# Expert weights in 2 MB units with 16 KB runs, and what that moves elsewhere in a two-block network

## The chip, the cores and the metric

The kernel runs on one core of a Trainium2 chip. The metric is the device time of one execution in microseconds (us). Before the change the median of three runs is 2280.82 us (2279.59 to 2280.99). All numbers are f32 in memory; products that choose experts are formed from a high and a low part of each weight, so that f32 accuracy is kept.

## The reference

256 tokens of width 1024 go through `first_block` (two layers of attention and feed-forward) and then `second_block` (a gated recurrence, a gated unit over chunks, a projection by `w_out`, and a layer of 16 experts), followed by a last RMSNorm. The change concerns the experts; each expert picks the 32 tokens with the largest share for it:

```python
def moe_expert_choice(h, router_w, w_gate, w_up, w_down):
    cap = CAPACITY_FACTOR * T // N_EXPERTS                      # 2 * 256 / 16 = 32
    aff = jax.nn.softmax((h @ router_w).astype(jnp.float32), axis=-1)
    gate, idx = lax.top_k(jnp.swapaxes(aff, 1, 2), cap)
    xs = h[bidx, idx]
    hid = jax.nn.silu(jnp.einsum('becd,edf->becf', xs, w_gate)) * jnp.einsum('becd,edf->becf', xs, w_up)
    ye = jnp.einsum('becf,efd->becd', hid, w_down) * gate[..., None].astype(h.dtype)
    return jnp.zeros_like(h).at[bidx, idx].add(ye)
...
        x = x + g_m * y                                         # y ends in the product by w_out
        h2 = modulate_2(rmsnorm_2(x, norm_ffn_w[l]), sh_f, sc_f)
        x = x + g_f * moe_expert_choice(h2, router_w[l], expert_w_gate[l], expert_w_up[l], expert_w_down[l])
    return rmsnorm_2(x, final_norm_w)
```

Each expert has three matrices of 8 MB (1024 x 2048, 1024 x 2048, 2048 x 1024): 403 MB in all, of 625 MB that the kernel moves.

## The kernel before

**Weights of everything but the experts.** `Weights` brings them in blocks of 1 MB into two buffers, `raw` (L101). ScalarE casts a block into `wh`, its high part (L396), VectorE forms `wl`, the low part, as the difference (L403), and TensorE multiplies with both (`mm3` and `gemm_T`; three matmuls per product, L485 to 487 and L503 to 505). The parts live in the pool `pair`, three buffers of `wh` and three of `wl`, 1 MB each. `more(n)` casts up to n blocks ahead and then calls `fetch(1)`, which may send one unit of expert weights.

**Expert weights.** `experts` lists them as 1 MB units in the order of use: for each expert eight k blocks of gate, eight of up, and eight of down. A unit of gate or up is 128 rows of 2048, one row (8 KB) to a partition; a unit of down is 256 rows, two rows (8 KB together) to a partition. The last four units, the second half of the last expert's down matrix, hold 512 columns each, in runs of 2 KB. `fetch` (DMA at L2196) goes round a ring of `slots`, which grows when other things are freed: `xw0` (4), `xw1` (2), then the two `raw` and six `pair` buffers, then `xw2` (5), 19 MB in all. While other weights still load, one unit goes out behind each `more`; when the last block of `w_out` has been taken, and again when the second block is done, `fetch()` sends all for which there is a slot. After that each `take()`, called before the matmuls of a unit, frees the slot of the unit before and sends one more.

All these DMAs, and those of `raw`, are sent by SyncE (SP) in program order, one after the other. SyncE waits, ahead of a DMA, for the semaphore of the one eight back and, where a buffer is written again, for its last reader.

**Ahead of the experts.** The end of the second block (`block2`) multiplies `merged` by `w_out` in four 1 MB blocks (kk, c), two token tiles each. `route` is a generator that is advanced between them. Its first step, `route_weights`, folds scale and shift into the router's weights on VectorE: `A2f` (the scale of the norm, 128 x 8, L658), `rb`, `rw` (L2223 to 2225). It is placed ahead of the first `w_out` product. After the last product come the router's logits, softmax, `moe`'s selection of 32 tokens for each expert, and `gather(0)`, which forms the first 512 features of all chosen tokens (`xsA`) by a product with a selection matrix `S`; scale and shift (`A2f` and a piece of `modc`) are applied where the result leaves PSUM. `gather(1)` forms the other half (`xB`) before the fifth k block of the first gate matrix.

**Experts.** For each unit of gate or up TensorE runs four matmuls (L2400), 32 tokens stationary, 512 columns of the unit moving, one for each quarter of the partitions of a PSUM bank, so that a bank holds 4 x 32 partitions of 512 columns. `columns` transposes the gated hidden layer back into columns, and L2418 (for the last four units L2428) multiplies with down. `scatter` adds an expert's output into the tokens while the next expert's gate runs. The hidden layer of the last expert is transposed twice, once for either way of reading down.

## Time and profile before

| | |
|---|---|
| median of three runs | 2280.82 us (2279.59 to 2280.99) |
| the profiled execution | 2285.08 us |
| its span, first to last instruction | 2283.2 us |
| mean granted clock of TensorE | 0.879 of full speed |
| TensorE busy | 1903.5 us, 83% |
| VectorE / ScalarE / GpSimd busy | 934.9 / 620.2 / 222.5 us |
| bytes moved | 625.48 MB in 182796 packets, mean 274 GB/s |
| the experts' DMAs | sent 19.8 to 19.9 us before they land, 1024 KB each |

The engines are PE (TensorE matmul), PEld (its weight load), DVE (VectorE), ACT (ScalarE), POOL (GpSimd) and SP (SyncE; SPq is its DMA queue). Busy shares are means over stages with different limits, so a stage is read by itself: by a window (busy time of each engine, granted clock and DMA in a stretch), by the timeline of an engine (instructions one after the other, with what ended the idle time before each), by the waits, and by the chain that ended last. [...]

### The profile page before, as it was taken

What the parts mean: (1) busy time and instruction counts of PE and PEld (TensorE: products, weight loads), DVE (VectorE), ACT (ScalarE), POOL (GpSimd) and SP (SyncE); (2) the same over time, 40 slices, a digit from 0 to 9 for tenths busy, and PEclk for the clock granted to TensorE, in tenths of its full rate; (3) what the DMA queues carried; (4) which work ended last, traced back from release to release, by engine and by line L of the source; (5) the groups of instructions that cost most, each with busy time, mean ns of one, the idle gap of its engine ahead of it and who ended that gap; (6) DMA issues with size and microseconds to landing.
All of it is one profiled execution on the core that took longest, in us unless ns stands there. A gap on an engine that the chain in (4) does not pass through costs nothing. (4 is left out here: it accounts for less than half of the span.)

```text
span 2283.2 us, 26558 instructions
## 1 busy us (share of the span) xinstructions
PE 1903.5 (83%) x10872; PEld 1166.0 (51%) x10872; DVE 934.9 (41%) x1400; ACT 620.2 (27%) x964; POOL 222.5 (10%) x282
## 2 busy tenths in 40 slices
PE   7999899999999999999979987676666666667665
PEld 4865688788778778999868751111111111111111
DVE  4547645687556765755578631000000000000001
ACT  3336433222134665644566420000000000000001
POOL 1001030111113001000242010000000000000000
PEclk8999999999999999999989987767777777777777
DMA  8446235776742234555434789999999999999998
GB/s 320 142 140 215 90 123 183 270 237 213 244 152 65 68 118 148 196 194 168 149 125 141 269 349 421 420 421 421 421 421 420 421 421 421 421 421 421 421 421 328
DMA packets 182796, 625.48 MB, mean 274 GB/s; under 512 B 17384, under 2 KB 77730, under 8 KB 130962
## 3 DMA queue, kind: packets, MB, share of 16 engines
q1 hardware_dynamic: 167792, 572.70, 64.9%
q0 software_dynamic: 14480, 50.63, 6.6%
q8 instruction: 86, 1.41, 0.3%
q10 hardware_dynamic: 402, 0.45, 0.1%
q14 instruction: 36, 0.29, 0.0%
HBM read 622.63 MB, written 1.10 MB: 273 GB/s over the span
## 5 line engine op out<-in xcount | busy, mean ns | idle before, releaser
L403 DVE TENSOR_TENSOR wl<-raw,wh 128x2048 fp32r<-128x2048 f32 (+3 forms) x141 | 293.1, 2083 | 234.4 <-ACT wh L396 231.4
L396 ACT CAST wh<-raw 128x2048 fp32r<-128x2048 f32 (+2 forms) x132 | 231.0, 1756 | 203.1 <-PE ps L504 102.2
L505 PE MATMUL ps<-hx,wl 128*128 128x256 f32 (+1 forms) x848 | 272.0, 321 | 3.9 <-DVE wl L403 3.8
L503 PE MATMUL ps<-hx,wh 128*128 128x256 f32 (+1 forms) x848 | 273.5, 323 | 0.0
L504 PE MATMUL ps<-lx,wh 128*128 128x256 f32 (+1 forms) x848 | 272.1, 321 | 0.9 <-DVE lx L720 0.7
L413 ACT COPY GT<-ps 128x256 f32<-128x256 f32 x16 | 6.0, 372 | 879.8 <-PE ps L2345 879.8
L2410 DVE TENSOR_TENSOR s<-s,gu 128x512 f32<-128x512 f32 x16 | 11.0, 687 | 478.0 <-ACT s L2409 478.0
L505 PEld LDWEIGHTS ps<-hx,wl 128*128 128x128 f32 x848 | 159.8, 188 | 17.2 <-DVE wl L403 4.8
L503 PEld LDWEIGHTS ps<-hx,wh 128*128 128x128 f32 x848 | 159.9, 189 | 14.7 <-issue 2.5
L504 PEld LDWEIGHTS ps<-lx,wh 128*128 128x128 f32 x848 | 159.9, 189 | 13.9 <-DVE lx L720 1.4
L2400 PE MATMUL gu<-xw,xB 128*32 128x512 f32 x584 | 107.2, 821 | 60.7 <-DMA xw<-in_expert_w_gate 30.7
L2400 PE MATMUL gu<-xw,xsA 128*32 128x512 f32 x584 | 106.9, 829 | 42.8 <-DMA xw<-in_expert_w_up 31.4
L2418 PE MATMUL ye<-xw,ehT 128*32 128x512 f32 x592 | 102.0, 812 | 47.1 <-DMA xw<-in_expert_w_down 39.3
L567 DVE SCALAR_TENSOR_TENSOR acc<-av,s,acc 128x1024 f32<-128x1024 f32 x84 | 106.1, 1281 | 40.2 <-DMA av<-in_ada_w 39.5
L2357 DVE TENSOR_TENSOR s<-gf,ye 128x512 f32<-128x512 f32 x32 | 20.6, 684 | 248.9 <-PE ye L2418 236.9
L485 PE MATMUL ps<-wh,hidh 128*128 128x512 f32 x264 | 104.3, 395 | 0.0
L487 PE MATMUL ps<-wh,hidl 128*128 128x512 f32 x264 | 103.7, 393 | 0.0
L486 PE MATMUL ps<-wl,hidh 128*128 128x512 f32 x264 | 103.5, 392 | 0.0
L2341 POOL TENSOR_TENSOR SG<-S,aff 128x128 f32<-128x128 f32 x32 | 12.1, 399 | 820.3 <-PE ps L2345 820.3
L2400 PEld LDWEIGHTS gu<-xw,xB 128*32 128x32 f32 x584 | 13.8, 123 | 147.1 <-DMA xw<-in_expert_w_up 79.7
L485 PE MATMUL ps<-wh,hx 128*128 128x512 f32 (+2 forms) x208 | 81.6, 392 | 6.9 <-ACT ST L1909 6.0
L486 PE MATMUL ps<-wl,hx 128*128 128x512 f32 (+2 forms) x208 | 79.9, 384 | 3.1 <-POOL wl L402 1.9
(566 smaller groups left out, 3258.2 us busy)
## 6 DMA issues: line engine op xcount, KB each, us to landing
xw<-in_expert_w_down SPq DMA_DIRECT2D x77, 1024.0 KB, 19.9
xw<-in_expert_w_gate SPq DMA_DIRECT2D x75, 1024.0 KB, 19.8
xw<-in_expert_w_up SPq DMA_DIRECT2D x71, 1024.0 KB, 19.8
raw<-in_ffn_w SPq DMA_DIRECT2D x64, 1024.0 KB, 5.1
av<-in_ada_w POOLq DMA_DIRECT2D x80, 512.0 KB, 5.2
raw<-in_w_in SPq DMA_DIRECT2D x28, 1024.0 KB, 5.1
araw<-in_ada_w SPq DMA_DIRECT2D x24, 1024.0 KB, 4.7
wl<-in_expert_w_up SPq DMA_DIRECT2D x22, 1024.0 KB, 19.9
```

Of the source, the lines that this page charges most:

```text
L396: self.nc.scalar.copy(hi, src)
L403: self.nc.vector.tensor_sub(lo[:, n:], src[:, n:], hi[:, n:].bitcast(F32))
L485: nc.tensor.matmul(o, lhsT=a, rhs=w[0][:, j, :], start=k0 + j == 0, stop=False)
L486: nc.tensor.matmul(o, lhsT=a, rhs=w[1][:, j, :], start=False, stop=False)
L487: nc.tensor.matmul(o, lhsT=b, rhs=w[0][:, j, :], start=False, stop=k0 + j == nk - 1)
L503: nc.tensor.matmul(out, lhsT=a, rhs=xh[:, k, n0:n0 + n], start=k == 0, stop=False)
L504: nc.tensor.matmul(out, lhsT=a, rhs=xl[:, k, n0:n0 + n], start=False, stop=False)
L505: nc.tensor.matmul(out, lhsT=b, rhs=xh[:, k, n0:n0 + n], start=False, stop=k == nk - 1)
L567: nc.vector.scalar_tensor_tensor(acc[r], w, s[:, k, r:r + 1], acc[r], op0=ALU.mult, op1=ALU.add)
L2357: nc.vector.tensor_tensor(y[c], gf[:, c * 512:(c + 1) * 512], ye[c], op=ALU.mult)
L2400: nc.tensor.matmul(ps[32 * j:32 * j + 32, :], lhsT=xsT[k // 4][:, k % 4, e * CAP:(e + 1) * CAP], rhs=w[:, j * 512:(j + 1) * 512], start=k ...
L2418: nc.tensor.matmul(ye[c][j:j + 32, :], lhsT=hT[:, 2 * (u % 2) + k, 32 * (u // 2):32 * (u // 2) + 32], rhs=w[:, k * 1024 + c * 512:k * 1024 ...
```

## The change

**Units.** A unit is 2 MB, two row blocks of before: a partition holds two neighbouring rows of gate or up, or four of down, 16 KB that lie together in memory. The slots are nine of 2 MB (`xw0` 2, `xw1` 1, `raw` 1, `pair` 3, `xw2` 2) and a buffer of 1 MB, `xh`, which takes the first half (columns 0 to 2047) of the unit for which there is no full slot yet; with it the bytes held are 19 MB as before. The `raw` slot is two buffers of 1 MB and takes two DMAs with runs of 8 KB. The last four units stay 1 MB with 2 KB runs. Since partition p now holds rows 2p and 2p+1, `gather` picks its features with a stride of two, `columns` with a stride of four, always, so that the last expert needs one transposition only. The scales and shifts must be in that order too: eight small matmuls in `route_weights`, with `ident` (a part of the constants, `ct`) as a moving or standing selector, put `A2f` and its shift into a bank, and VectorE copies them to `fAB`.

**Pieces.** While other weights load (`fetch(1)`), a 2 MB unit goes out as two DMAs of 64 partitions, one call of `fetch` each.

**Pairs.** The high and low part of a block are two halves of one 2 MB tile `w`, so that they share one buffer.

```diff
-NX = 4, 2, 5
+NX = 2, 1, 2
...
-            hi = k.pair.tile([P, 2048], F32R, tag="wh", name="wh")
-            lo = k.pair.tile([P, 2048], F32R, tag="wl", name="wl")
+            hi, lo = k.pair_tiles()
...
-        return (self.pair.tile([P, 2048], F32R, tag="wh", name="wh"), self.pair.tile([P, 2048], F32R, tag="wl", name="wl"))
+        t = self.pair.tile([P, 4096], F32R, tag="w", name="w")
+        return t[:, :2048], t[:, 2048:]
...
-                    self.slots += [(self.raw, "raw")] * NRAW + [(self.pair, "wh"), (self.pair, "wl")] * 3
+                    self.slots += [(self.raw, "raw")] + [(self.pair, "w")] * 3
                     self.fetch()
...
+        self.half, self.first, self.pieces = None, None, []
...
         for e in range(16):
             for W in (Wg, Wu):
-                for k in range(KD):
-                    self.units.append(W[e][k * P:(k + 1) * P, :])
-            for u in range(8 if e < 15 else 4):
-                self.units.append(Wd[e][u * 256:(u + 1) * 256, :].rearrange("(p k) n -> p (k n)", k=2))
+                for b in range(4):
+                    self.units.append(W[e][b * 256:(b + 1) * 256, :].rearrange("(p k) n -> p (k n)", k=2))
+            for f in range(4 if e < 15 else 2):
+                self.units.append(Wd[e][f * 512:(f + 1) * 512, :].rearrange("(p k) n -> p (k n)", k=4))
...
-            self.slots += [(self.pool(f"xw{i}", NX[i]), "xw")] * NX[i]
+            pl = self.pool(f"xw{i}", NX[i])
+            self.slots += [(pl, "xw")] * NX[i]
+            if i == 2:
+
+                self.half = pl.tile([P, 2048], F32, tag="xh", name="xh", bufs=1)
 
     def fetch(self, n=1000):
 
-        w = self.w
-        while n and self.fetched < min(self.used + len(self.slots), len(self.units)):
+        w, dma = self.w, self.nc.sync.dma_start
+        few = n < 1000
+        while n:
+            n -= 1
+            if self.pieces:
+                dma(*self.pieces.pop(0))
+                continue
             i = self.fetched
-            n -= 1
+            if i >= min(self.used + len(self.slots), len(self.units)):
+                break
             pl, tag = self.slots[i % len(self.slots)]
             if tag == "raw" and w.issued < len(w.items) or pl is self.pair and w.taken < len(w.items):
                 return
             src = self.units[i]
-            t = pl.tile([P, 2048], F32, tag=tag, name=tag)
-            d = t.rearrange("p (k n) -> p k n", k=src.shape[1]) if len(src.shape) > 2 else t
-            if i < len(self.units) - 1:
-                self.nc.sync.dma_start(d, src)
+            if len(src.shape) > 2:
+                t = [pl.tile([P, 2048], F32, tag=tag, name=tag)]
+                d = t[0].rearrange("p (k n) -> p k n", k=src.shape[1])
+                if i < len(self.units) - 1:
+                    dma(d, src)
+                else:
+                    for k in range(src.shape[1]):
+                        dma(d[:, k, :], src[:, k, :])
+            elif self.first is not None:
+                t = [self.first, pl.tile([P, 2048], F32, tag=tag, name=tag)]
+                self.first = None
+                dma(t[1], src[:, 2048:])
+            elif tag == "raw":
+                t = [pl.tile([P, 2048], F32, tag=tag, name=tag) for _ in range(2)]
+                for k in range(2):
+                    dma(t[k], src[:, k * 2048:(k + 1) * 2048])
             else:
-                for k in range(src.shape[1]):
-                    self.nc.sync.dma_start(d[:, k, :], src[:, k, :])
+                x = pl.tile([P, 4096], F32, tag=tag, name=tag)
+                t = [x[:, :2048], x[:, 2048:]]
+                if few:
+
+                    dma(x[:64], src[:64])
+                    self.pieces.append((x[64:], src[64:]))
+                else:
+                    dma(x, src)
             self.live.append(t)
             self.fetched += 1
+        if self.half is not None and self.fetched == len(self.slots):
+            self.first, self.half = self.half, None
+            dma(self.first, self.units[self.fetched][:, :2048])
         if len(self.units) == self.fetched < self.used + len(self.slots) and self.fn is None:
             pl, tag = self.slots[self.fetched % len(self.slots)]
             self.fn = pl.tile([P, 1024], F32, tag=tag, name="fn")
-            self.nc.sync.dma_start(self.fn, self.io["final_norm_w_2"].partition_broadcast(P))
+            dma(self.fn, self.io["final_norm_w_2"].partition_broadcast(P))
...
         nc.vector.tensor_tensor(rw, rw, b(self.fA), op=ALU.mult)
+
+        ps = self.bank()
+        for i, x in enumerate((self.fA, self.mod(2, 3, 0))):
+            for j in range(2):
+                for h in range(2):
+                    nc.tensor.matmul(ps[64 * h:64 * h + 64, 8 * i + 4 * j:8 * i + 4 * j + 4], lhsT=self.ident[:, j:P:2],
+                                     rhs=x[:, h:8:2], start=True, stop=True)
+        self.fAB = self.rp.tile([P, 2, 8], F32, name="fAB")
+        nc.vector.tensor_copy(self.fAB.rearrange("p i (b j) -> p i j b", j=2), ps[:, :16].rearrange("p (i j b) -> p i j b", i=2, j=2))
...
-        x, aff, A, B = self.xres, self.aff, self.fA, self.mod(2, 3, 0)
+        x, aff = self.xres, self.aff
+        A, B = self.fAB[:, 0], self.fAB[:, 1]
...
-                        nc.tensor.matmul(ps, lhsT=xp[c][:, i, t, d * P:(d + 1) * P], rhs=S[:, t].rearrange("p e s -> p (e s)"),
+                        nc.tensor.matmul(ps, lhsT=xp[c][:, i, t, 256 * (d // 2) + d % 2:256 * (d // 2 + 1):2], rhs=S[:, t].rearrange("p e s -> p (e s)"),
...
-        def columns(sg, n):
+        def columns(sg):
 
 
             pt = self.bank("pt")
-            for i in range(4):
-                h = 256 * (i // n) if n < 4 else 0
-                nc.tensor.transpose(pt[:, i * P:(i + 1) * P], sg[:, h + i % n:h + n * P:n], self.ident)
+            for k in range(4):
+                nc.tensor.transpose(pt[:, k * P:(k + 1) * P], sg[:, k:4 * P:4], self.ident)
...
-                for k in range(KD):
+                for k in range(4):
                     w = self.take()
-                    if e + i == 0 and k == 4:
+                    if e + i == 0 and k == 2:
                         xsT.append(self.t([P, 4, 512], "xB", 1, pool=mp))
                         gather(1)
-                    for j in range(4):
-                        nc.tensor.matmul(ps[32 * j:32 * j + 32, :], lhsT=xsT[k // 4][:, k % 4, e * CAP:(e + 1) * CAP],
-                                         rhs=w[:, j * 512:(j + 1) * 512], start=k == 0, stop=k == KD - 1)
-                    if late and k == 1:
+                    for h in range(2):
+                        for j in range(4):
+                            nc.tensor.matmul(ps[32 * j:32 * j + 32, :], lhsT=xsT[k // 2][:, 2 * (k % 2) + h, e * CAP:(e + 1) * CAP],
+                                             rhs=w[h][:, j * 512:(j + 1) * 512], start=k + h == 0, stop=k + h == 4)
+                    if late and k == 0:
...
-            for u in range(4 if last else 8):
+            for f in range(2 if last else 4):
                 w = self.take()
-                for k in range(2):
-                    for c in range(2):
-                        j = 32 * (2 * k + (c + u) % 2)
-                        nc.tensor.matmul(ye[c][j:j + 32, :], lhsT=hT[:, 2 * (u % 2) + k, 32 * (u // 2):32 * (u // 2) + 32],
-                                         rhs=w[:, k * 1024 + c * 512:k * 1024 + c * 512 + 512], start=u < 2, stop=u >= 6)
+                for c in range(2):
+                    for k in range(4):
+                        n = k % 2 * 1024 + c * 512
+                        nc.tensor.matmul(ye[c][32 * k:32 * k + 32, :], lhsT=hT[:, k, 32 * f:32 * f + 32],
+                                         rhs=w[k // 2][:, n:n + 512], start=f == 0, stop=f == 3)
...
-            hT = columns(sg, 4)
...
-                    w = self.take()
+                    w, = self.take()
```

SyncE's queue at the end of the second block, as a piece of the difference. `raw` are blocks of other weights, `xw` the slots for units of experts; L2225 of the changed kernel sends the first 64 partitions of a unit, L2195 the other 64.

```order
 L101 DMA raw<-in_w_in 128x4x512
-L2196 DMA xw<-in_expert_w_gate 128x2048
+L2225 DMA xw<-in_expert_w_gate 64x4096
 L101 DMA raw<-in_w_branch_a 128x4x512
-L2196 DMA xw<-in_expert_w_gate 128x2048
+L2195 DMA xw<-in_expert_w_gate 64x4096
 L101 DMA raw<-in_w_out 128x4x512
-L2196 DMA xw<-in_expert_w_gate 128x2048
+L2225 DMA xw<-in_expert_w_gate 64x4096
 L101 DMA raw<-in_w_out 128x4x512
-L2196 DMA xw<-in_expert_w_gate 128x2048
+L2195 DMA xw<-in_expert_w_gate 64x4096
```

At each place of a DMA of 128 partitions with rows of 2048 stands one of 64 partitions with rows of 4096; the `raw` blocks and their number are the same.

TensorE before, where the last product of the branch ends (`kq` is its right-hand side) and the first product by `w_out` begins (`wh`, `wl` are the block's parts, `hx`, `lx` those of the merged rows):

```order
L485 MATMUL ps<-wh,kq 128x512
L486 MATMUL ps<-wl,kq 128x512
L487 MATMUL ps<-wh,kq 128x512
L485 MATMUL ps<-wh,hx 128x512 [waits Activation_49]
L486 MATMUL ps<-wl,hx 128x512 [waits DVE_49]
L487 MATMUL ps<-wh,lx 128x512
```

And in the changed kernel (`w` is either part; L484 to 486 are the lines 485 to 487 of before; `ct` holds the identity):

```order
L484 MATMUL ps<-w,kq 128x512
L485 MATMUL ps<-w,kq 128x512
L486 MATMUL ps<-w,kq 128x512
L2263 MATMUL ps<-A2f,ct 64x4 [waits DVE_49]
L2263 MATMUL ps<-A2f,ct 64x4 x3
L2263 MATMUL ps<-modc_101,ct 64x4 x4
L484 MATMUL ps<-w,hx 128x512 [waits Activation_49]
L485 MATMUL ps<-w,hx 128x512
L486 MATMUL ps<-w,lx 128x512
```

Eight matmuls, four on `A2f` and four on its shift in `modc_101`, stand between the two products, and the first waits for VectorE.

VectorE before, in the same place (`wl<-raw,wh` is the low part of a block of `w_out`, of 128x2048 elements; `lx<-ps,hx` that of merged rows):

```order
L403 TENSOR_TENSOR wl<-raw,wh 128x2048 [waits DMAHW2_49,Activation_49]
L658 SCALAR_TENSOR_TENSOR A2f<-modc_101,colC 128x8
L2223 TENSOR_TENSOR rb<-rw,modc_101 128x128 [waits DMASW0_49]
L2224 TENSOR_REDUCE rbs<-rb 128x16 [waits DVE_49]
L2225 TENSOR_TENSOR rw<-rw,A2f 128x128
L403 TENSOR_TENSOR lx<-ps,hx 128x512 [waits Activation_49]
```

And in the changed kernel:

```order
L402 TENSOR_TENSOR w<-raw,w 128x2048 [waits DMAHW2_49,Activation_49]
L657 SCALAR_TENSOR_TENSOR A2f<-modc_101,colC 128x8
L2255 TENSOR_TENSOR rb<-rw,modc_101 128x128 [waits DMASW0_49]
L2256 TENSOR_REDUCE rbs<-rb 128x16 [waits DVE_49]
L2257 TENSOR_TENSOR rw<-rw,A2f 128x128
L2266 COPY fAB<-ps 128x2x2x4 [waits PE_49]
L402 TENSOR_TENSOR lx<-ps,hx 128x512 [waits Activation_49]
```

`A2f` stands behind the low part of a block in both. Behind `rw` one copy, which waits for TensorE, is new, and all that follows stands one place later.

## Rows read from the trace of the kernel before

**Rows 1.** Page, bytes moved, in 40 equal slices of the span.
```profile
GB/s 320 142 140 215 90 123 183 270 237 213 244 152 65 68 118 148 196 194 168 149 125 141 269 349 421 420 421 421 421 421 420 421 421 421 421 421 421 421 421 328
```

**Rows 2.** Chain that ended last, in order of time: start us, length us, what.
```profile
1364.82 20.86 DMA wh<-in_expert_w_gate
1385.75 19.86 DMA xw<-in_expert_w_up
...
2246.15 20.27 DMA xw<-in_expert_w_down
```

**Rows 3.** Waits of SyncE's queue: line, releaser, total us, times, longest us.
```profile
SPq L2196 <- DMA xw<-in_expert_w_up: 145.4, 68, 3.5
...
SPq L2196 <- PE gu L2400: 25.3, 11, 17.0
```

**Rows 4.** Windows: stretch, length, PE PEld DVE ACT POOL busy (x), PEclk, DMA share, GB/s.
```profile
1345.00:1350.00 5.00, 5.00 (x12) 3.77 (x13) 3.29 (x6) 0.00 (x0) 0.00 (x0) 0.53 0.93 392
1350.00:1353.00 3.00, 3.00 (x25) 1.24 (x27) 1.35 (x2) 1.56 (x2) 0.00 (x0) 1.00 0.06 22
```

**Rows 5.** TensorE timeline: start us, length us, instruction, [idle before <- releaser].
```profile
1306.27 0.40 PE L485 MATMUL ps<-wh,hx 128*128 128x512 f32 x1
...
1333.61 1.96 PE L2250 MATMUL ps<-rw,ga 128*128 128x16 f32 x16 [0.25 <-ACT ga L2245]
...
1351.05 3.64 PE L2400 MATMUL gu<-xw,xsA 128*32 128x512 f32 x32
```

**Rows 6.** Windows of the stream of expert weights and of its end.
```profile
1400.00:1600.00 200.00, 137.13 (x692) 27.08 (x692) 17.61 (x26) 3.48 (x8) 3.02 (x8) 0.71 1.01 421
...
2258.00:2266.00 8.00, 6.51 (x44) 1.74 (x36) 0.00 (x0) 0.58 (x1) 0.00 (x0) 0.81 1.04 387
```

**Rows 7.** Page, DMA queue: packets, MB, share of 16 engines.
```profile
q8 instruction: 86, 1.41, 0.3%
```

**Rows 8.** Window in which two 64-partition halves of `ab_w_out` move.
```profile
103.00:107.00 4.00, 4.00 (x25) 2.82 (x18) 0.69 (x1) 0.32 (x1) 0.00 (x0) 1.00 1.07 216
```

**Rows 9.** Window ahead of the `w_out` products.
```profile
1285.00:1302.00 17.00, 17.00 (x79) 13.74 (x78) 10.84 (x9) 8.96 (x10) 0.00 (x0) 1.00 0.98 367
```

**Rows 10.** SyncE timeline, DMA issues there; columns as in rows 5.
```profile
1284.61 0.50 SPq L2196 DMA_DIRECT2D xw<-in_expert_w_gate  x1
...
1288.46 0.39 SPq L2196 DMA_DIRECT2D xw<-in_expert_w_gate  x1
...
1293.94 0.46 SPq L2196 DMA_DIRECT2D xw<-in_expert_w_gate  x1
1300.90 5.65 SPq L101 DMA_DIRECT2D raw<-in_w_out  x2
```

**Rows 11.** ScalarE timeline, cast of the third `w_out` block.
```profile
1307.10 1.91 ACT L396 CAST wh<-raw 128x2048 fp32r<-128x2048 f32 x1 [2.31 <-DMA raw<-in_w_out]
```

**Rows 12.** VectorE timeline, its low part and `A2f`.
```profile
1309.05 2.29 DVE L403 TENSOR_TENSOR wl<-raw,wh 128x2048 fp32r<-128x2048 f32 x1 [0.24 <-ACT wh L396]
1311.26 0.16 DVE L658 SCALAR_TENSOR_TENSOR A2f<-modc,colC 128x8 f32<-128x8 f32 x1
```

**Rows 13.** Windows of an idle stretch of TensorE and of what follows it.
```profile
1257.00:1261.00 4.00, 2.16 (x11) 1.31 (x10) 4.00 (x6) 0.53 (x2) 0.00 (x0) 0.99 0.58 171
1261.00:1264.00 3.00, 3.00 (x16) 3.00 (x15) 2.26 (x2) 0.00 (x0) 0.00 (x0) 0.50 1.05 430
```

**Rows 14.** TensorE timeline: a unit in the stream, and the last one.
```profile
1398.18 1.94 PE L2400 MATMUL gu<-xw,xsA 128*32 128x512 f32 x8 [1.41 <-DMA xw<-in_expert_w_up]
...
2266.47 1.07 PE L2428 MATMUL ye<-xw,ehT 128*32 128x512 f32 x8 [1.28 <-DMA xw<-in_expert_w_down]
```

**Rows 15.** Waits of TensorE: group, releaser, total us, times, longest us.
```profile
PE ps L505 <- DVE wl L403: 3.8, 3, 1.5
```

More of the change, by code (lines that the diff above doesn't have):

```diff
@@ L968, in part @@
             raw, (_, kt, n, _) = w.raws.pop(0), w.items[w.issued - 1]
-            hl = [self.pair.tile([P, 2048], F32R, tag=x, name=x) for x in ("wh", "wl")]
+            hl = self.pair_tiles()
             def steps():
@@ L2410, in moe @@
             nc.vector.tensor_tensor(sg, sg, gu[1], op=ALU.mult)
-            hT = columns(sg, 2)
+            hT = columns(sg)
             ye = [self.bank("ye") for _ in range(2)]
-            for u in range(4 if last else 8):
+            for f in range(2 if last else 4):
                 w = self.take()
-                for k in range(2):
-                    for c in range(2):
-                        j = 32 * (2 * k + (c + u) % 2)
-                        nc.tensor.matmul(ye[c][j:j + 32, :], lhsT=hT[:, 2 * (u % 2) + k, 32 * (u // 2):32 * (u // 2) + 32],
-                                         rhs=w[:, k * 1024 + c * 512:k * 1024 + c * 512 + 512], start=u < 2, stop=u >= 6)
+                for c in range(2):
[3 more added lines that the diff above has]
+                                         rhs=w[k // 2][:, n:n + 512], start=f == 0, stop=f == 3)
             if not last:
```

## The prediction

> **What bounds the kernel now.** I read the slices of the span first. From the 25th of 40 on, the DMA engines move 420 to 421 GB/s without a break, up to the last slice [rows 1]: about 900 us in which nothing but the rate of this stream counts. The chain of waits says the same: from 1364.82 to 2266.47 us every step is the landing of one 1 MB unit of expert weights, each some 19.9 us after its issue [rows 2]. 19.9 us is eight units of 2.49 us each: SyncE sends a unit when the one eight back has landed, and hardly ever waits for a free buffer there (longest two rows of its waits, [rows 3]). So the end is set by two things: **when the stream starts without a break, and its rate**. Before 1364 us the chain does not run through DMA: the DMA engines stand nearly still from 1350 to 1353 us, at 22 GB/s [rows 4], because all 19 MB of buffers are full (at 392 GB/s in the five us before, the last of them lands at about 1349.6) and the first one comes free only when TensorE's first expert matmuls, which start at 1351.05 [rows 5], have read it. Up to there TensorE and the routing behind it are the path; whatever delays them delays the stream's restart one for one, and with it the end.
>
> **Part 1: longer runs, the rate.** The rate depends on the run per descriptor. With 8 KB runs the engines move 421 GB/s; at the end, where the last four units have 2 KB runs, 387 GB/s with engines just as full [rows 6]. Per engine (a sixteenth), a packet of 8 KB takes 16 x 8192 / 421 = 311.3 ns, one of 2 KB 84.7 ns. A straight line through both has 36.9 ns per 1000 bytes and 9.2 ns per packet. A 16 KB packet then takes 9.2 + 604.3 = 613.5 ns: 427.3 GB/s. Per MiB that is 2.4540 in place of 2.4907 us, 0.0367 us less. Of the 365 MB after the restart some 40 MB go to the buffer that still takes two DMAs of 8 KB runs (every ninth unit), and 4.5 MB keep their short runs; 321 MB gain: 321 x 0.0367 = **-11.8 us**. No row shows a 16 KB packet of these queues; 16 KB packets exist (86 packets, 1.41 MB, queue 8, [rows 7]). Bounds: 0 if a 16 KB run gains nothing over 8 KB, and -24 us if the whole 9.2 ns went away (434 GB/s); a loss is excluded by the trend of the two rows. I take the line, since the 8 KB row is the nearest and lies on it.
>
> [...]
>
> **Part 2: pieces of 64 partitions.** While other weights load, a unit goes out as two DMAs of 64 partitions, 1 MB each, at the places where a 1 MB unit of 128 partitions stood. The kernel before already has such DMAs: the halves of `ab_w_out` at 103 to 107 us move 216 GB/s with the engines full [rows 8]. At that rate 1 MiB takes 4.85 us in place of 2.49: +2.36 us each. There are eight pieces. The first three meet no block that is needed soon, and the last two are counted in part 4. Pieces four to six (where before units went at 1284.61, 1288.46 and 1293.94) fall into a stretch in which the engines are full, 1285 to 1302 us, 367 GB/s at 98% [rows 9, 10]; the queue drains 3 x 2.36 = 7.1 us later, at 1309 instead of 1302. Behind it stands the third block of `w_out`. Before, it was issued at 1300.90 and cast by ScalarE as soon as it had landed, at 1307.10 [rows 10, 11]; now it follows the queue: 1309 + 2.7 for its bytes at 387 GB/s + some 1.3 for the landing to be seen (an estimate, from the 3.5 us that the way from issue to cast took beside the bytes) = 1313, **5.8 us later**. As such this is harmless: TensorE needs that block only two blocks, some 11 us, after the first.
>
> **Part 3: the eight new matmuls.** They reorder two columns of scales into `fAB`, and stand on TensorE ahead of the first `w_out` product, which ran at 1306.27 [rows 5]. They wait for `A2f`. On VectorE `A2f` stands behind the low part of the third `w_out` block, which began at 1309.05, and so ran only at 1311.26, for 0.16 us [rows 12]. TensorE, dense before, therefore waits from 1306.27 to 1311.42: 5.15 us, and with part 2 5.8 more: **10.95 us**. Queued behind it is everything up to the routing and the gather, and for that SyncE's pair buffers, freed by TensorE. Own time: sixteen matmuls 16 columns wide take 1.96 us [rows 5], so eight take **0.98**. After an idle of a few us the granted clock stood at 0.50 from 1261 to 1264 us [rows 13], the lower level; some 3.2 us of resumed work at half speed cost **1.6**. Bounds of these: 5.15 if part 2 does not reach VectorE, 12.3 if all its 7.1 us do; clock 0 to 2.4.
>
> **Part 4: buffers of 2 MB.** The preload stays 19 MB (nine units and a half). Its last pieces add 4.7 us, which fills the idle 3 us at 1350; counted from that side, the preload ends at 1349.6 + 13.5 + 4.7 = 1367.8 while the first slot comes free at 1366.4, so the two sides agree within about 1 us. The first slot comes free after two k blocks in place of one: TensorE took 3.64 us for four [rows 5], so **+0.91**. [...] The dropped second transposition of the last expert is off the path: the matmul behind it waited 1.28 us for DMA anyway [rows 14]. Nothing there.
>
> **Part 5: pairs in one tile.** ScalarE may begin a cast only when both old parts are read: one matmul (0.3 us) later than now. TensorE waited only three times, 3.8 us, for VectorE's part on the commonest line [rows 15]; 0 to 2.5 us, and a gain is not excluded by VectorE's dropped waits; I take **+0.3**.
>
> Sum: -11.8 + 10.95 + 0.98 + 1.6 + 0.91 + 0.3 = **+2.9 us**. On the profiled execution: 2285.08 to 2288.0, of which the span 2283.2 to 2286.1. That execution is 4.3 us above the median of the runs, 2280.82; on the median I forecast **2283.7 us**, no change that can be told: 0.2% is 4.6 us, about what a measurement here can tell from no change.
>
> **The rivals.** *Longer runs gain nothing.* If the engines or the descriptor writers cut 16 KB into two, or the 2 KB row is slow for another reason (its rows lie 4 KB apart), part 1 is zero and only the start remains: +14.7 us, 2295.5, slower. It decides in the stream: with the start as above, any rate below 426.4 GB/s (a gain of 10.1 us) already puts the time more than 0.2% above. Against it: 387 to 421 is a rise. [...]
> *The pieces delay nobody*, because they are not half as fast or the queue has slack: 5.15 in place of 10.95, sum -2.9, 2277.9. Against it: the 216 GB/s row.
> *The start delay is swallowed whole*, if TensorE's wait only replaces later ones: the sum is then -11 to -12, 2270, faster. Against it: TensorE is full in that stretch and the chain of waits runs through the routing.
>
> **How the numbers follow.** Forecast 0.58 (own range 2277 to 2290: 0.39 within 0.2%, 0.16 slower, 0.03 faster); no gain from runs 0.14, slower; pieces without delay 0.16 (0.10 within, 0.06 faster); swallowed 0.12, faster. Together faster 0.21, same 0.49, slower 0.30. The range 2273 to 2293 leaves out rather more than half of the two outer rivals, 0.16, and little else.
>
> **What would show it.** In the stream: GB/s (427 right; 421 the first rival) and 2 MB landings 4.9 us apart. At 1306 to 1320: a TensorE wait for VectorE's `A2f` of about 11 us (5 for the second rival). First expert matmul near 1364.6 instead of 1351.05 (below 1354: the third). Pieces at about 215 GB/s. I am wrong if the DMA engines wait for buffers within the stream, which SyncE's waits would show as releases by TensorE.

## The result

The changed kernel takes **2296.76 us** (median of six runs, 2287.24 to 2302.53); the kernel before, run beside it, 2280.90 (2279.59 to 2285.27). The ratio is 1.0061, 95% interval [1.0047, 1.0075]: slower, by some 14 us by the ratio and by 15.9 by the two medians, where 2283.7 and at most 2293 were forecast. The profiled execution took 2294.06 us with a span of 2292.3.

The chain that ended last in the changed kernel (start us, length us, what):

```profile
1369.93 3.57 PE gu L2442 x32
1373.50 3.92 PE ps L2370 x16
1377.42 10.44 PE gu L2442 x96
...
1397.94 27.62 DMA xw<-in_expert_w_up
1425.62 34.34 DMA xw<-in_expert_w_gate
1460.02 34.34 DMA w<-in_expert_w_down
...
2240.36 35.30 DMA xw<-in_expert_w_down
```

The shape is that of [rows 2]: TensorE up to the first experts, then nothing but landings. So the kernel still has two parts that add, a start and a stream. First the stream, by windows (stretch, length, busy us and instructions of PE, PEld, DVE, ACT, POOL, granted clock, DMA share, GB/s):

```profile
1400.00:1600.00 200.00, 129.37 (x738) 30.25 (x726) 20.66 (x30) 2.62 (x6) 2.28 (x6) 0.79 1.01 426
2000.00:2200.00 200.00, 118.36 (x690) 27.13 (x682) 16.51 (x24) 2.62 (x6) 2.28 (x6) 0.83 1.01 426
```

426 GB/s against 421 in [rows 6]; 427.3 were forecast. The loss is at the start. TensorE's timeline there (start us, length us, instruction, and the idle time before it with what ended it):

```profile
1300.86 0.40 PE L486 MATMUL ps<-w,kq 128*128 128x512 f32 x1
1322.09 0.60 PE L2263 MATMUL ps<-A2f,ct 128*64 128x4 f32 x8 [20.83 <-DVE A2f L657]
1323.04 0.80 PE L484 MATMUL ps<-w,hx 128*128 128x512 f32 x1
1323.63 0.63 PE L485 MATMUL ps<-w,hx 128*128 128x512 f32 x1
...
1369.86 3.64 PE L2442 MATMUL gu<-xw,xsA 128*32 128x512 f32 x32
```

The eight matmuls wait 20.83 us for `A2f`, not 10.95. During the wait the granted clock falls to 0.50 of full speed, and it stays there up to 1327.4 us (matmuls of 0.63 us in place of 0.40), and the first expert matmul starts 69.0 us after the last product of the branch (1369.86 - 1300.86). In the kernel before it was 45.0 us, from the branch's last product to 1351.05 in [rows 5]:

```profile
1306.04 0.39 PE L487 MATMUL ps<-wh,kq 128*128 128x512 f32 x1
```

What `A2f` waits for is seen on ScalarE and VectorE, which prepare the blocks of `w_out` (same columns):

```profile
1299.51 1.91 ACT L395 CAST w<-raw 128x2048 fp32r<-128x2048 f32 x1 [7.42 <-DMA raw<-in_w_out]
...
1311.89 1.90 ACT L395 CAST w<-raw 128x2048 fp32r<-128x2048 f32 x1 [9.02 <-DMA raw<-in_w_out]
...
1317.73 1.90 ACT L395 CAST w<-raw 128x2048 fp32r<-128x2048 f32 x1 [2.98 <-DMA raw<-in_w_out]
```

```profile
1319.66 2.29 DVE L402 TENSOR_TENSOR w<-raw,w 128x2048 fp32r<-128x2048 f32 x1 [0.90 <-ACT w L395]
1321.87 0.16 DVE L657 SCALAR_TENSOR_TENSOR A2f<-modc,colC 128x8 f32<-128x8 f32 x1
```

All three blocks come late. Measured from the first product by `w_out` or the wait in front of it, the third cast was at +0.83 us before (1307.10 in [rows 11] against 1306.27) and is at +16.47 now (1317.73 against 1301.26): 15.6 us later, where 5.8 were forecast.

One thing about the profile of before has to be known to read this: in its execution, 4.3 us above the median, the branch ended at 1306; in nine of the eleven other traces of this study it ended between 1300 and 1304. Some of that difference is there long before the first DMA of expert weights: the table load of ScalarE that starts at 974.5 us in e1's trace starts at 981.1 in e5's. So times are compared from the branch's end on, in two parts: X, from the branch's last product to the first expert matmul, and Y, from there to the end of the span. Both are read from TensorE's timeline and the span of each trace. The medians come from four sets of runs, each with its own runs of the kernel before (2280.9 to 2283.0); the ratios below compare within a set.

| kernel | median us | X us | Y us |
|---|---|---|---|
| before | 2280.9 to 2283.0 | 45.0 | 932.2 |
| changed | 2296.8 | 69.0 | 922.4 |
| e1: matmuls late, narrow pieces | 2289.0 | 60.8 | 923.0 |
| e2: wide pieces, matmuls in place | 2281.9 | 54.5 | 922.5 |
| e3: both | 2271.4 | 44.8 | 921.6 |
| e4: before, with the matmuls | 2291.3 | 51.6 | 934.0 |
| e5: e3 with runs of 8 KB | 2285.4 | 45.2 | 935.5 |
| e6: e1 with every second partition | 2272.6 | 45.1 | 922.0 |
| e7: e3 with whole units | 2272.6 | 45.1 | 922.4 |
| e8: before, with the pair tile | 2280.7 | 44.8 | 932.3 |
| e9: narrow pieces 1 to 4 | 2287.9 | 60.4 | 922.5 |
| e10: narrow pieces 5 to 8 | 2288.6 | 62.2 | 924.6 |

The change costs 24.0 us in X and gains 9.7 us in Y: +14.3, about what the ratio says. All experiments fall into this scheme: Y is 922 to 925 with 16 KB runs and 932 to 936 with 8 KB, and X is 45 wherever neither the matmuls nor the narrow pieces are in the way.

### The profile page after: what moved, and what is told of

It is laid out like the page before. It is cut to its first block, busy times and chain, and to the rows that moved or that the text cites. A ratio compares the mean times of both kernels' runs of the same rounds, so it can differ in the third digit from the quotient of the medians.

```text
span 2292.3 us, 26247 instructions
## 1 busy us (share of the span) xinstructions
PE 1838.1 (80%) x10884; PEld 1173.4 (51%) x10884; DVE 936.2 (41%) x1401; ACT 619.5 (27%) x963; POOL 223.3 (10%) x282
## 5 line engine op out<-in xcount | busy, mean ns | idle before, releaser
L402 DVE TENSOR_TENSOR w<-raw,w 128x2048 fp32r<-128x2048 f32 (+3 forms) x141 | 293.1, 2083 | 252.9 <-ACT w L395 250.1
L395 ACT CAST w<-raw 128x2048 fp32r<-128x2048 f32 (+2 forms) x132 | 230.9, 1756 | 226.9 <-PE ps L504 103.7
L504 PE MATMUL ps<-hx,w 128*128 128x256 f32 (+1 forms) x848 | 272.0, 321 | 3.6 <-DVE w L402 3.4
L502 PE MATMUL ps<-hx,w 128*128 128x256 f32 (+1 forms) x848 | 273.5, 323 | 0.0
L503 PE MATMUL ps<-lx,w 128*128 128x256 f32 (+1 forms) x848 | 272.1, 321 | 0.9 <-DVE lx L719 0.7
L504 PEld LDWEIGHTS ps<-hx,w 128*128 128x128 f32 x848 | 159.8, 188 | 16.9 <-DVE w L402 4.5
L502 PEld LDWEIGHTS ps<-hx,w 128*128 128x128 f32 x848 | 159.8, 188 | 14.6 <-issue 2.1
L503 PEld LDWEIGHTS ps<-lx,w 128*128 128x128 f32 x848 | 159.9, 189 | 13.9 <-DVE lx L719 1.4
L484 PE MATMUL ps<-w,hidh 128*128 128x512 f32 x264 | 104.5, 396 | 0.0
L486 PE MATMUL ps<-w,hidl 128*128 128x512 f32 x264 | 103.7, 393 | 0.0
L485 PE MATMUL ps<-w,hidh 128*128 128x512 f32 x264 | 103.3, 391 | 0.0
L2442 PE MATMUL gu<-w,xB 128*32 128x512 f32 x336 | 55.7, 796 | 49.6 <-DMA w<-in_expert_w_up 30.7
L484 PE MATMUL ps<-w,hx 128*128 128x512 f32 (+2 forms) x208 | 82.3, 396 | 6.9 <-ACT ST L1909 6.0
```

Of the source, the lines that this page charges most:

```text
L395: self.nc.scalar.copy(hi, src)
L402: self.nc.vector.tensor_sub(lo[:, n:], src[:, n:], hi[:, n:].bitcast(F32))
L484: nc.tensor.matmul(o, lhsT=a, rhs=w[0][:, j, :], start=k0 + j == 0, stop=False)
L485: nc.tensor.matmul(o, lhsT=a, rhs=w[1][:, j, :], start=False, stop=False)
L486: nc.tensor.matmul(o, lhsT=b, rhs=w[0][:, j, :], start=False, stop=k0 + j == nk - 1)
L502: nc.tensor.matmul(out, lhsT=a, rhs=xh[:, k, n0:n0 + n], start=k == 0, stop=False)
```

## The experiments

Two theories on X stood against each other: W, that only TensorE's wait for `A2f` is the loss, and P, that the blocks come late because of the pieces of 64 partitions ("narrow" below; "wide" are 128 partitions with half the columns) and would cost that time anyway.

**e1, the matmuls moved from `route_weights` behind the router's last products:**

```diff
-        ps = self.bank()
-        for i, x in enumerate((self.fA, self.mod(2, 3, 0))):
...
         for t in range(2):
             products(t, 1)
+        pf = self.bank()
+        for i, x in enumerate((self.fA, self.mod(2, 3, 0))):
...
         nc.vector.tensor_tensor(aff, aff, b, op=ALU.mult)
+        self.fAB = self.rp.tile([P, 2, 8], F32, name="fAB")
```

> The changed kernel with its eight matmuls on the scales moved behind the router's last products, and the copy to fAB to the end of the router; pieces of 64 partitions stay. Theory W (TensorE's wait for A2f is the loss at the start, 20.83 us in the changed kernel's trace): that wait is gone and nothing takes its place, the first expert matmul comes at about 1350 instead of 1369.86, and the time is some 10 us below the kernel before (2271). Theory P (the blocks of w_out come late because of the pieces, so the wait only moves): TensorE waits about 2.5 us for the first block and 6 to 7 us for the second (its low part was done at 1303.7 and 1316.1 in the changed kernel, where TensorE ends the products before it at 1301.3), the first expert matmul comes at about 1356 to 1358, and the time is 2 to 5 us below the kernel before (2276 to 2279). If neither is the cause, 2290 to 2297 as the changed kernel.

Measured: 2289.0 us, ratio 1.0022 [1.0003, 1.0041]. Theory W falls: 8 us come back, not 25. P has the direction, but its 2276 to 2279 were too low. TensorE's timeline of this kernel shows why:

```profile
1303.86 0.50 PE L485 MATMUL ps<-w,hx 128*128 128x512 f32 x1 [1.83 <-DVE w L402]
...
1318.13 0.45 PE L731 MATMUL ps<-ct,ga 128*128 128x128 f32 x1 [8.64 <-DVE ga L2122]
1319.37 0.90 PE L731 MATMUL ps<-ct,ga 128*128 128x128 f32 x3 [0.79 <-DVE ga L2122]
...
1361.87 3.64 PE L2442 MATMUL gu<-xw,xsA 128*32 128x512 f32 x32
```

And VectorE's:

```profile
1314.37 2.29 DVE L402 TENSOR_TENSOR w<-raw,w 128x2048 fp32r<-128x2048 f32 x1 [9.97 <-ACT w L395]
1316.58 0.68 DVE L2121 TENSOR_TENSOR ga<-ga,ps 128x512 f32<-128x512 f32 x1
```

And ScalarE's:

```profile
1312.44 1.90 ACT L395 CAST w<-raw 128x2048 fp32r<-128x2048 f32 x1 [9.51 <-DMA raw<-in_w_out]
1314.24 1.05 ACT L2117 ACTIVATE ga<-ga 128x1024 f32<-128x1024 f32 x1
```

TensorE waits little for the late block itself (1.83 us); the long wait is for `ga`, the gated branch that it is to transpose next. All that `ga` is made of was there at 1302.9 us, when ScalarE had copied its second half. But its sigmoid (L2117) stands on ScalarE behind the cast of the second block, which came at 1312.44, and its product on VectorE behind that block's low part. 1.83 + 8.64 + 0.79 = 11.3 us of waits, and the lower clock behind them (0.50 of full speed from 1314 to 1322 us), make most of the 15.8 us that X is longer than before.

**e2, wide pieces, matmuls in place, and e3, both mends:**

```diff
-                    dma(x[:64], src[:64])
-                    self.pieces.append((x[64:], src[64:]))
+                    dma(x[:, :2048], src[:, :2048])
+                    self.pieces.append((x[:, 2048:], src[:, 2048:]))
```

> The changed kernel with pieces of 128 partitions and half the columns (8 KB runs), at the same places in the queue; the eight matmuls stay where they are. Theory P (pieces of 64 partitions move at about half the rate and push the blocks of w_out back by 10.6 us): VectorE's A2f comes back to about 1306 to 1311 and TensorE's wait for it shrinks from 20.8 to between 5 and 6 us measured against the kernel before (5 to 10 in the trace, as TensorE arrives earlier or not); the first expert matmul some 8 us later than in the kernel before in place of 18.8, and the time 2 us below to 1 us above the kernel before (2279 to 2282). If the number of partitions does not matter, 2290 to 2297 as the changed kernel.

> The changed kernel with both: matmuls on the scales late, and pieces of 128 partitions with 8 KB runs. What is left is the stream with 16 KB runs and one first slot of two k blocks. If the two causes are the whole loss at the start, the first expert matmul is within 2 us of that of the kernel before, and the time is 9 to 11 us below it (2270 to 2272, ratio 0.995 to 0.996). If the 2 MB buffers themselves cost something at the start (the ring is filled later, or the first slot comes free later), 2273 to 2280.

Measured: e2 2281.9 us, ratio 1.0002 [0.9992, 1.0012]; e3 **2271.4 us**, ratio 0.9955 [0.9940, 0.9969], both as expected. e3 is faster than either kernel. TensorE's wait in e2, and e3's first expert matmul:

```profile
1307.98 0.60 PE L2263 MATMUL ps<-A2f,ct 128*64 128x4 f32 x8 [5.65 <-DVE A2f L657]
```

```profile
1347.68 3.64 PE L2442 MATMUL gu<-xw,xsA 128*32 128x512 f32 x32
```

With these four kernels X is a square: 44.8 with neither, +9.7 by the matmuls alone, +16.0 by the narrow pieces alone, +24.2 by both. So the two nearly add: all but 1.5 us of one shows beside the other.

**e4, the kernel before with the eight matmuls and the copy alone** (their result is not used):

```diff
         nc.vector.tensor_tensor(rw, rw, b(self.fA), op=ALU.mult)
+        ps = self.bank()
+        for i, x in enumerate((self.fA, self.mod(2, 3, 0))):
...
+        self.fAB = self.rp.tile([P, 2, 8], F32, name="fAB")
```

> The kernel before, to which only the eight matmuls and the copy are added, where the changed kernel has them; their result is not used. If TensorE's wait for A2f passes to the end one for one: 5.15 us of wait, 0.95 us for the matmuls and about 2 us at the lower clock behind the idle, together 8 us, 2289 (ratio 1.0035). If the start's delay is swallowed by the transfers (3 us of idle DMA at 1350 and a full ring), 0 to 3 us, 2281 to 2284.

Measured: 2291.3 us, ratio 1.0045 [1.0029, 1.0061]. TensorE, ScalarE and SyncE of this kernel:

```profile
1305.26 0.41 PE L2230 MATMUL ps<-A2f,ct 128*64 128x4 f32 x8 [4.39 <-DVE A2f L658]
```

```profile
1314.21 1.91 ACT L396 CAST wh<-raw 128x2048 fp32r<-128x2048 f32 x1
```

```profile
1305.16 13.65 SPq L2196 DMA_DIRECT2D raw<-in_expert_w_gate  x2
1319.77 0.33 SPq L2196 DMA_DIRECT2D wh<-in_expert_w_up  x1
```

The wait is 4.39 us, X grows by 6.6, and the median is later by 10: it is not swallowed. The 6.6 us are 4.39 of wait, 0.58 for the matmuls and 1.66 for the products of the first block, which begin at the lower clock (0.57 of full speed from 1306 to 1310 us, 1.00 from there). Another 1.9 us lie in Y, where this execution's stream ran at 420 GB/s in place of 421. The last two fences show a second path that the prediction did not have: ScalarE casts the fourth block (1314.21) only behind casts of `hx` that wait for TensorE, so its `raw` buffer comes free late, and SyncE needs 13.65 us for the two DMAs to `raw`. All of the preload is queued behind it. In e3 the pair takes 6.20 us, in the changed kernel 14.46:

```profile
1308.21 6.20 SPq L2219 DMA_DIRECT2D raw<-in_expert_w_gate  x2
```

```profile
1303.77 12.74 SPq L101 DMA_DIRECT2D raw<-in_w_out  x2
1321.98 14.46 SPq L2219 DMA_DIRECT2D raw<-in_expert_w_gate  x2
1337.38 0.47 SPq L2225 DMA_DIRECT2D w<-in_expert_w_up  x1
```

This path adds nothing to X in e4, since the three terms make up the 6.6 us without it and no DMA is what the first expert matmul waits for. That it costs time anywhere is not shown.

**e5, e3 with a unit of 2 MB read as two runs of 8 KB per partition:** the same DMAs, buffers and order; features stay in their natural order, and the last expert is transposed twice again, as before the change.

```diff
-                    self.units.append(W[e][b * 256:(b + 1) * 256, :].rearrange("(p k) n -> p (k n)", k=2))
+                    self.units.append(W[e][b * 256:(b + 1) * 256, :].rearrange("(k p) n -> p k n", k=2))
...
-                    dma(x, src)
+                    dma(x.rearrange("p (k n) -> p k n", k=2), src)
```

> The version with both mends (matmuls on the scales late, pieces of 128 partitions; 2271.4), but a unit of 2 MB is read as two runs of 8 KB to a partition in place of one of 16 KB, with the same DMAs, buffers and order of use; the features then lie in their natural order. Theory R (the rate in the stream hangs on the run per descriptor): 420 to 421 GB/s in the stream instead of 426, and some 10 us more, 2281 to 2282. If the 426 GB/s come from DMAs of twice the size or from fewer of them, 426 GB/s and 2270 to 2273.

Measured: 2285.4 us, ratio 1.0017 [1.0006, 1.0027]. The stream's windows:

```profile
1400.00:1600.00 200.00, 122.47 (x684) 28.33 (x684) 17.91 (x26) 3.48 (x8) 3.02 (x8) 0.82 1.01 420
2000.00:2200.00 200.00, 122.23 (x687) 28.64 (x682) 17.92 (x26) 3.48 (x8) 3.02 (x8) 0.79 1.01 420
```

X is that of e3 within 0.4 us and Y 13.9 us longer; the 365 MB after the restart (MB of 1048576 bytes) take 12.8 us more at 420 than at 426 GB/s. DMAs of 2 MB with 8 KB runs move no more (420 GB/s) than those of 1 MB (421, [rows 6]): here the rate belongs to the run, not to the size or the number of DMAs. The medians of e5 and e3 are 14.0 us apart, as Y is; some 10 were expected, so the gain of the long runs had been put too low there, and about 1 us of Y is not accounted for. By itself the 2 MB unit gives nothing: with 8 KB runs, and X as before, the ratio is 1.0017.

**e6, pieces of every second partition** (otherwise e1):

```diff
-                    dma(x[:64], src[:64])
-                    self.pieces.append((x[64:], src[64:]))
+                    dma(x[0:P:2], src[0:P:2])
+                    self.pieces.append((x[1:P:2], src[1:P:2]))
```

> The kernel of the first experiment (matmuls on the scales late, 2289.0), but a piece is every second partition (0, 2, ... and 1, 3, ...) in place of the lower and the upper 64. If a piece is slow because it writes to one half of the partitions only: the blocks of w_out come in time, and the time is that of pieces of 128 partitions with 8 KB runs, 2270 to 2274. If it is slow because it has 64 descriptors of 16 KB, wherever they go: 2286 to 2291 as the first experiment, with DMA engines full at 160 to 280 GB/s from 1255 to 1311 us.

Measured: 2272.6 us, ratio 0.9968 [0.9956, 0.9980]: as fast as wide pieces. The windows of 1285 to 1302 us, ahead of the `w_out` products, first of e6, then of e1, then of the changed kernel (columns as above; before it was 367 GB/s, [rows 9]):

```profile
1285.00:1302.00 17.00, 17.00 (x78) 13.74 (x77) 10.15 (x10) 9.51 (x9) 0.00 (x0) 1.00 1.00 388
```

```profile
1285.00:1302.00 17.00, 16.97 (x76) 13.19 (x75) 5.30 (x6) 4.82 (x5) 0.00 (x0) 1.00 0.99 202
```

```profile
1285.00:1302.00 17.00, 16.26 (x74) 12.80 (x73) 4.58 (x5) 4.88 (x5) 0.00 (x0) 1.00 1.01 224
```

The engines are full in all three, at 388 or at 202 and 224 GB/s. The pieces of e6 also have 64 packets of 16 KB. They differ in where they go, and also in what they read: every second 16 KB in place of 1 MB in a row. The kernel before settles which of the two counts, since its units read 1 MB in a row to all 128 partitions and run at full rate (421 GB/s, [rows 6]). So what makes a piece slow here is that it goes to one contiguous half of the partitions.

The time of single packets, averaged over those that start in a stretch, tells the pieces from the blocks of 2 KB runs that move beside them. The last column is what 16 engines would move if all packets took that long:

| trace, stretch (us) | packets | ns each | GB/s |
|---|---|---|---|
| before, 1255 to 1311 | 8 KB, units | 313 | 419 |
| | 2 KB, blocks | 96 | 343 |
| e6, 1285 to 1302 | 16 KB, pieces | 620 | 423 |
| | 2 KB, blocks | 91 | 361 |
| e1, 1285 to 1302 | 16 KB, pieces | 1290 | 203 |
| | 2 KB, blocks | 159 | 206 |
| changed, 1255 to 1311 | 16 KB, pieces | 1263 | 208 |
| | 2 KB, blocks | 123 | 267 |

A packet to one half took twice as long (1290 ns in e1 and 1263 in the changed kernel against 620 in e6; 203 to 208 GB/s against 423), and the blocks, which go to all partitions, were slowed beside it (159 and 123 ns against 91). Why one half takes longer is not shown.

**e7, whole units of 2 MB in place of two pieces** (otherwise e3):

```diff
-                dma(*self.pieces.pop(0))
+                self.pieces.pop(0)
...
-                    dma(x[:, :2048], src[:, :2048])
-                    self.pieces.append((x[:, 2048:], src[:, 2048:]))
+                    dma(x, src)
+                    self.pieces.append(None)
```

> The version with both mends (2271.4), but while other weights load, a 2 MB unit goes out whole (128 partitions, 16 KB runs) at the place of its first piece, and nothing at that of the second. Same bytes ahead of each block of w_out but for the order. If only the rate of the pieces matters, no difference that can be told: 2269 to 2273. If a block queued behind 2 MB comes up to 2.5 us later and TensorE waits for it, up to 2276.

Measured: 2272.6 us, ratio 0.9965 [0.9955, 0.9976]. No difference to e3 (2271.4 us) that can be told: with wide pieces it did not matter whether a unit goes out in two (286 GB/s from 1255 to 1311 us here, 281 in e3).

**e8, the pair tile alone, in the kernel before:**

```diff
-            hi = k.pair.tile([P, 2048], F32R, tag="wh", name="wh")
-            lo = k.pair.tile([P, 2048], F32R, tag="wl", name="wl")
+            hi, lo = k.pair_tiles()
...
-        self.slots += [(self.raw, "raw")] * NRAW + [(self.pair, "wh"), (self.pair, "wl")] * 3
+        self.slots += [(self.raw, "raw")] * NRAW + [(self.pair, "w")] * 6
```

> The kernel before with the pair tile alone: high and low part of a block share one 2 MB buffer, expert units stay 1 MB and use its halves. The prediction took 0.3 us for this, between 0 and 2.5: 2280 to 2284, ratio 1.000 to 1.001. If ScalarE's cast, now released only when both old parts have been read, is late at many of the blocks, 2284 to 2290.

Measured: 2280.7 us, ratio 1.0000 [0.9989, 1.0011]. No cost of the pair tile can be told; X and Y are those of the kernel before within 0.3 us.

**e9 and e10, only the first or only the last four pieces narrow** (otherwise the changed kernel; e10 has `i >= 2` where e9 has `i < 2`):

```diff
                 if few:
-                    dma(x[:64], src[:64])
-                    self.pieces.append((x[64:], src[64:]))
+                    if i < 2:
+                        dma(x[:64], src[:64])
+                        self.pieces.append((x[64:], src[64:]))
+                    else:
+                        dma(x[:, :2048], src[:, :2048])
+                        self.pieces.append((x[:, 2048:], src[:, 2048:]))
```

> The changed kernel (2296.8), but only the first four pieces (those sent at about 1255 to 1280 us, ahead of the blocks of w_out) have 64 partitions; the others have 128 partitions and 8 KB runs. The matmuls on the scales stay in place, so that the wait for A2f shows a delay of the blocks. As the prediction had it (these pieces meet nothing that is needed soon, but for the fourth): 2282 to 2285, close to the 2281.9 with no narrow piece. If they fill the gaps of the queue and what is sent behind them inherits the delay: A2f waits over 8 us and the time is 2286 to 2293.

> The changed kernel (2296.8), but only the last four pieces (two sent between the blocks of w_out, at about 1284 and 1294 us, two in the preload behind) have 64 partitions; the first four have 128 partitions and 8 KB runs. As the prediction had it (the pieces next to the blocks of w_out do the harm): most of the 14.9 us that separate the changed kernel from the one without narrow pieces, 2290 to 2296. If it is the backlog from the first four: 2282 to 2287.

Measured: e9 2287.9 us, ratio 1.0025 [1.0014, 1.0037]; e10 2288.6 us, ratio 1.0026 [1.0016, 1.0036]. TensorE's wait in e9, the blocks on ScalarE in e9, and the wait in e10:

```profile
1320.10 0.59 PE L2267 MATMUL ps<-A2f,ct 128*64 128x4 f32 x8 [12.09 <-DVE A2f L657]
```

```profile
1296.55 1.91 ACT L395 CAST w<-raw 128x2048 fp32r<-128x2048 f32 x1 [8.43 <-DMA raw<-in_w_branch_a]
1303.60 1.90 ACT L395 CAST w<-raw 128x2048 fp32r<-128x2048 f32 x1 [4.66 <-DMA raw<-in_w_out]
```

```profile
1314.07 0.60 PE L2267 MATMUL ps<-A2f,ct 128*64 128x4 f32 x8 [13.41 <-DVE A2f L657]
```

Against 5.65 us with no narrow piece (e2) the wait grows by 6.4 with the first four, by 7.8 with the last four, and by 15.2 with all eight. e9's median is where the backlog was expected to put it; e10's lies between its two forecasts, so neither set of pieces does the harm alone. Of e10's four pieces the last two were sent behind the wait (1329.76 and 1330.28 us), so two pieces made its 7.8 us.

In e9 no narrow piece stands between the blocks of `w_out`, yet ScalarE waits 8.43 us for the branch's block ahead of them, and the delay is handed on. There TensorE even waits inside the branch, which X leaves out; this profiled execution is 4.4 us above e9's median.

```profile
1298.51 0.49 PE L484 MATMUL ps<-w,kq 128*128 128x512 f32 x1 [0.92 <-ACT w L395]
1300.84 0.49 PE L485 MATMUL ps<-w,kq 128*128 128x512 f32 x1 [1.83 <-DVE w L402]
```

Windows of 1276 to 1282 us, ahead of the branch's last block, show the backlog: in e3, in the first row, the engines stand still, and in e9 they are full.

```profile
1276.00:1282.00 6.00, 6.00 (x27) 4.80 (x27) 3.14 (x3) 4.75 (x5) 0.00 (x0) 1.00 0.00 0
```

```profile
1276.00:1282.00 6.00, 6.00 (x27) 4.83 (x26) 3.12 (x3) 3.34 (x4) 0.00 (x0) 1.00 1.08 269
```

By its packets the third piece of e9, sent at 1268.98 us, moved only from 1277.5 to 1287.8; the branch's block was sent at 1281.00, behind it.

## Why the prediction was wrong, by its own steps

**Part 1, the rate: right.** 426 GB/s against a forecast of 427.3 from a straight line through two packet sizes; Y is 9.7 us shorter in the changed kernel and 10.5 in e3, against a forecast of -11.8 for the rate and +0.91 for the first slot, together -10.9. In e5 the gain goes with the run (420 GB/s at 8 KB). Packet by packet, in the stream from 1400 to 2200 us, an 8 KB packet took 314 ns before and a 16 KB packet 617 ns in the changed kernel; the straight line had 311.3 and 613.5. Nothing comes from the size of a DMA: with 8 KB runs those of 2 MB moved 420 GB/s (e5) and those of 1 MB 421 ([rows 6]). The first rival, that longer runs gain nothing, is out.

**Part 2, the pieces: the step that failed.** The kind of effect was right, its size was not: +5.8 us for the third block of `w_out` (5.9 by the rounded numbers of its own sum), measured 15.6. The rate of the pieces was not the error. It was taken as 216 GB/s from [rows 8], and the packets of the changed kernel's pieces ran at 208. Three other things were. First, only the pieces were slowed in the sum. The blocks beside them were slowed too, from 96 to 123 ns for a packet of 2 KB. Windows of 1255 to 1311 us, of the kernel before and of the changed kernel, and the end of this stretch in the changed kernel:

```profile
1255.00:1311.00 56.00, 53.89 (x263) 44.42 (x262) 36.17 (x35) 27.89 (x28) 3.19 (x4) 0.97 0.72 266
```

```profile
1255.00:1311.00 56.00, 44.98 (x230) 36.93 (x230) 26.00 (x28) 20.49 (x22) 1.99 (x2) 0.93 1.01 238
...
1304.00:1311.00 7.00, 0.00 (x0) 0.00 (x0) 0.34 (x1) 0.00 (x0) 0.00 (x0) 0.50 0.94 177
```

The engines were 72% busy before and are full now, and move less. Second, "the first three meet no block that is needed soon" left out the backlog. Only three pieces were counted, 7.1 us; by the packet times a piece took 5.05 us of all engines (64 packets of 1263 ns, by 16) in place of 2.50, so six took some 15 us more and the slowed blocks some 6 (an estimate: 3432 packets of 2 KB, 27 ns longer each, by 16), of which the gaps of before take up a part. e9 has narrow only the first three and the fourth, which the sum counted at 2.36 us; its wait grew by 6.4 us, TensorE waited ahead of it too, and the third piece was still moving when the branch's block was sent. Third, the prediction drained the queue once, as if only bytes counted. But there are two `raw` buffers: a block that lands late is cast late, its low part is formed late, and only then may SyncE send the block after next; SyncE sent the third block of `w_out` at 1303.77, as the first one's low part was done (1301.45 + 2.29), and it was cast 14 us later. The landing of these blocks tells it in one row of the DMA issues (the changed kernel, then e3; before it was 8.4 us):

```profile
raw<-in_w_out SPq DMA_DIRECT2D x4, 1024.0 KB, 16.1
```

```profile
raw<-in_w_out SPq DMA_DIRECT2D x4, 1024.0 KB, 7.4
```

So the term was +5.8 and measured 15.6 (third cast) to 16.0 (X, e1 against e3). How the 15.6 us divide among the three is not measured. "As such this is harmless", because TensorE needs the third block only two blocks later, was wrong too: e1 takes the wait for `A2f` away and X is still 15.8 us longer than before, since the second block is late as well and `ga` stands behind its cast and its low part.

**Part 3, the matmuls: right in kind, near in size.** The place costs 5.15 us by the prediction, 5.65 in e2 and 4.39 in e4. Own time 0.95 (1322.09 to 1323.04) against 0.98. The clock: the 24 products of the first block took 7.7 us in place of 5.6, so 2.1 more, where 1.6 was forecast. Alone the matmuls cost 6.6 us (e4) to 9.7 us (e2) of X, against 7.7; e2 waits longer than e4 and runs longer at the lower clock behind it, 0.50 of full speed (matmuls of 0.63 us up to 1314 us, in e4 up to 1309). The SyncE path that e4 shows was not in the sum, and no cost of it is shown.

**Parts 4 and 5: right as far as the runs tell.** The preload lands as the first expert matmul starts, so that neither side waits long for the other, the stream's windows have full engines, and no cost of the pair tile can be told (e8). The window ahead of the first expert matmul of the changed kernel:

```profile
1360.00:1370.00 10.00, 6.60 (x22) 4.89 (x26) 7.39 (x15) 0.81 (x2) 0.00 (x0) 0.58 1.01 426
```

Put together with the measured sizes, 5.15 + 15.7 (the rest of the 20.83) + 0.95 + 2.1 = 23.9 us for X, measured 24.0, and -9.7 for Y: +14.2 in place of +2.9. One term, the pieces, makes 9.9 of the 11.3 us that were missed between the two traces. The rivals "pieces delay nobody" and "swallowed whole" are refuted by e2 and e4; a rival in which the pieces cost more than the queue's bytes, which is what happened, was not on the list, and the range ended 3.8 us short of the median.

## What to carry to other kernels

When a queue with few buffers is slowed down, cost the delay along the loop buffer, cast, low part, next issue, and look for what stands in order behind the late item on each engine it passes; bytes over rate gave only a lower bound here. A small instruction that is put ahead of a large batch on a full engine must have all its inputs ready there: eight matmuls of 0.95 us cost 6.6 to 9.7, and placed behind the router's products they cost nothing that X shows (e3). If a transfer has to be cut, cut it by columns or by every second partition, not into a lower and an upper half (2271.4 us in e3 and 2272.6 in e6 against 2289.0 in e1).

## What the runs showed of the hardware

Not expected: 64 partitions were as fast as 128 when they were spread (a 16 KB packet took 620 ns in e6, and 617 in the changed kernel's stream, which goes to 128), and half as fast when they were contiguous (1290 ns in e1). A slow piece also slowed the packets of other DMAs that moved beside it: those of 2 KB took 159 ns in e1 and 91 in e6.

Runs of 2, 8 and 16 KB gave 387, 420 to 421 and 426 GB/s with full engines; at 8 KB it made no difference whether a DMA moved 1 MB or 2 MB. What stays open: the runs of the changed kernel lie 15 us apart (2287 to 2302) and those of e1 13.5, those of e3 2.5 us; only one execution of each was profiled, so it isn't shown which wait varies. How much the SyncE path of e4 would cost, were TensorE's path shorter, is open too.
